# Keys of one residue modulo 16 copied side by side by GpSimd, ahead of the logit products of dilation 16

## The chip, the core and the metric

The kernel runs on one core of one Trainium2 chip. The metric is the device time of one execution in microseconds (us). The kernel before took 2262.62 us, the median of three runs (2255.15 to 2264.13). The profiled execution took 2264.64 us, of which 2262.8 us lie between its first and its last instruction.

## The reference, cut to what matters

One layer of an encoder for 4096 tokens of width 1024. The normalised input is projected; half of the width goes through a gated convolution of width 3, the other half through attention with 8 heads of 64. The attention is what the change touches:

```python
DILATED_CONFIGS = ((128, 1), (512, 4), (2048, 16))   # window, dilation
# for each: query i attends to the keys i + dilation*j, |j| <= 64
logits = einsum('bhnqd,bhnkd->bhnqk', qr, kblk) * dh**-0.5
p = exp(logits + bias - max)
o = p @ v / sum(p)
# the three results are mixed by a softmax over their log-sum-exps
```

For a dilation `d` the sequence is split into `d` residue classes. Within one class the pattern is a band of half-width 64, swept in blocks of 128 queries that see 256 keys (192 at the first and the last block of a class). A class of dilation 16 has 256 tokens, so it is two blocks, and each of them sees 192 keys.

## The kernel before, in words

The kernel has three parts. The first projects x to queries, keys, values and gates, with 512-column matmuls (L385 to L387), and writes them to device memory. The second, from about 793 us to 1903 us, runs the attention together with the convolution's projections, and the third joins the three dilations and multiplies with the output weights.

In the second part the attention is cut into 384 **units**: a pair of heads (4 pairs), a dilation, a quarter (`grp`, 4 of them) and a block of 128 queries (`b`, 8 of them). For each pair of heads 32 units of dilation 16 come first, then 32 of dilation 1 and 32 of dilation 4 (for the last pair, 4 and then 1). Such 32 units in a row are called a **stage** here; there are twelve stages, four of them of dilation 16.

The order of all work is written out by hand: the loop from L1098 issues for each unit, on all engines, a slice of a pipeline, and each engine executes its instructions in that order. In the iteration of unit `u`:

- `p_hi` and `p_lo` (L1026, L1038) split the probabilities of `u` into two f16 parts on ScalarE and VectorE. For even units a DMA transposes them (`tr`, L1048); for odd units TensorE has transposed them before (`tr_pe`, L1019), and the columns that a block of 192 keys leaves empty are zeroed by GpSimd (L994, L1035).
- `exps(u + 1)` on ScalarE (L1003).
- `fill` (L844) issues the convolution's matmuls (L809 to L811, 128x256), so many steps for each unit by a fixed plan (`pers`). The convolution's gate is a GpSimd multiply (L775) that waits for VectorE (L774).
- `av(u - 3)` (L1052) multiplies probabilities and values, 12 matmuls of 64 columns (L1061 to L1063).
- `q_alone(u + 5)` (L968): GpSimd copies the queries of one head of the pair, 64x128, into a tile `qz` whose other half is zero (two copies, L973). The tile was last used by unit `u + 1`, so the copy waits for that unit's products.
- `qk(u + 2)` (L975): four matmuls, L985 and L986 for each head of the pair. The 128 queries are loaded as weights; the keys are the moving operand. L985 takes the packed tile of queries and one part of the keys, L986 takes `qz` and another part of the keys.
- `logits(u + 2)` (L989): VectorE adds the bias and takes the maximum.
- For units of dilation 1 `q_order` (L952) has GpSimd put queries in order (128x256, L958).

Queries and keys of a pair of heads lie in five tiles `qk_t` of 128x4096 f16, filled by transposing DMAs in four chunks of 1024 columns (L615); tiles 0 and 1 hold queries, 2 to 4 keys. Their columns are sorted by residue modulo 4. So the keys of a unit of dilation 4 lie side by side, those of dilation 1 in runs of 32, and those of dilation 16 are read with a step of 4 elements, which is 8 bytes:

```python
step, at = (4, grp * (S // 4) + b // 2) if d == 16 else (1, grp * (S // 4))
U["kc"] = (at + step * (128 * n - (0 if lead else 64)), [[step, U["kn"]]])
```

The queries of dilation 16 have the same step (`U["qc"]`), as weights in L985 and as input of the copies L973.

Of the kernel before, what the change touches and what calls it, by code (L numbers as in the profile page):

```python
# [20 lines left out]
F16 = mybir.dt.float16  # L21
# [8 lines left out]
S = 4096  # L30
# [27 lines left out]
QZB = 4  # L58
# [7 lines left out]
def tile_hybrid_block(  # L66
# [14 lines left out]
    nc = tc.nc  # L81
# [24 lines left out]
    def bank(n, shape, dt=F32):  # L106
        return ps.tile(shape, dt, name=f"bank{n % 8}")
# [497 lines left out]
    pb = phB.enter_context(tc.tile_pool(name="pb", bufs=1))  # L605
    qk_t = [pb.tile([128, S], F16, name=f"qk{j}") for j in range(3)]
# [237 lines left out]
    def fill(n):  # L844
        state["owed"] += n
        while state["owed"] >= 1.0 and not state["done"]:
            state["owed"] -= 1.0
            if bg:
                bg.pop(0)()
            if todo:  # L850
                todo.pop(0)()
            try:
                next(dense)
            except StopIteration:
                state["done"] = True
# [30 lines left out]
    def load_v(pr, g, grp):  # L886
        d = DILS[g]
        vt = pb.tile([128, 9, 256], F16, name="vt", bufs=2)
        up, dn = slice(64, 128), slice(0, 64)
        if d == 16:  # L890
            nc.scalar.dma_start(vt[up, 0:4, :], v_rows(pr, grp, [[16 * VR, 64], [4 * VR, 4], [1, 256]]))
            nc.scalar.dma_start(vt[:, 4:8, :], v_rows(pr, 16 * 64 + grp, [[16 * VR, 128], [4 * VR, 4], [1, 256]]))
            nc.scalar.dma_start(vt[dn, 0:4, :], v_rows(pr, 16 * 192 + grp, [[16 * VR, 64], [4 * VR, 4], [1, 256]]))
        elif d == 4:
            nc.scalar.dma_start(vt[up, 0:8, :], v_rows(pr, grp, [[4 * VR, 64], [512 * VR, 8], [1, 256]]))
            nc.scalar.dma_start(vt[dn, 1:9, :], v_rows(pr, 4 * 64 + grp, [[4 * VR, 64], [512 * VR, 8], [1, 256]]))

            nc.scalar.dma_start(vt[dn, 0, :], v_rows(pr, grp, [[4 * VR, 64], [1, 256]]))
            nc.scalar.dma_start(vt[up, 8, :], v_rows(pr, grp, [[4 * VR, 64], [1, 256]]))
        else:  # L900
            for r in range(4):
                rows = slice(32 * r, 32 * r + 32)
                n = 8 if grp in (0, 3) else 9
                tok = 1024 * grp + (64 if grp == 0 else -64) + r
                nc.scalar.dma_start(vt[rows, int(grp == 0):int(grp == 0) + n, :], v_rows(pr, tok, [[4 * VR, 32], [128 * VR, n], [1, 256]]))
                if n == 8:
                    tok = (S - 128) * (grp == 3) + r
                    nc.scalar.dma_start(vt[rows, 8 * (grp == 3), :], v_rows(pr, tok, [[4 * VR, 32], [1, 256]]))
        return vt
# [3 lines left out]
    units = []  # L913
    for gi, (pr, g, grp) in enumerate(groups):
        d = DILS[g]
        for b in range(8):
            if d == 16:
                n, nb = b % 2, 2
                vidx = (b // 2 + 4 * n, b // 2 + 4 * (1 - n))
            elif d == 4:  # L920
                n, nb, vidx = b, 8, (b, b + 1)
            else:
                n, nb, vidx = 8 * grp + b, 32, (b, b + 1)
            lead, last = n == 0, n == nb - 1
            U = dict(pr=pr, g=g, d=d, grp=grp, gi=gi, b=b, vidx=vidx, kn=256, c0=0)
            if d == 1:

                U["qc"] = (128 * (b % 2), [[1, 128]])
                U["kc"] = (16, [[-16, 2]]) if lead else (32 * n, [[-16, 2]]) if last else (32 * n - 16, [[32, 2]])
                U["kc"][1].extend([[S // 4, 4], [1, 32]])  # L930
                U["b0"] = 256 if lead else 0 if last else 128
                if lead or last:
                    U["vidx"] = (b + 1, b)
            else:
                step, at = (4, grp * (S // 4) + b // 2) if d == 16 else (1, grp * (S // 4))
                U["qc"] = (at + step * 128 * n, [[step, 128]])
                U["kn"] = 256 - 64 * lead - 64 * last
                U["kc"] = (at + step * (128 * n - (0 if lead else 64)), [[step, U["kn"]]])
                U["b0"] = U["c0"] = 64 if lead else 0
            units.append(U)  # L940
    VT, OT, ST, PT = {}, {}, {}, {}
# [4 lines left out]
    def cols(t, at, rows=None):  # L946
        t = t if rows is None else t[rows]
        return bass.AP(tensor=t.tensor, offset=t.offset + at[0], ap=[list(t.ap[0])] + at[1])
# [14 lines left out]
    QZ = [[pb.tile([128, 128], F16, name=f"qz{n}_{i}") for i in range(2)] for n in range(QZB)]  # L963
# [4 lines left out]
    def q_alone(u):  # L968
        U = units[u]
        q_t = QN[u // 2] if U["d"] == 1 else qk_t  # L970
        for i in range(2):
            half = slice(64 * i, 64 * i + 64)
            nc.gpsimd.tensor_copy(QZ[u % QZB][i][half], cols(q_t[i], U["qc"], half))  # L973

    def qk(u):  # L975
        U = units[u]
        if U["b"] == 0:
            OT[U["gi"]] = pb.tile([128, 8, 2, DH + 2], F32, name="ot", bufs=2)
        kn = U["kn"]
        both = bank(3 + u % 2, [128, 2, 256])  # L980
        p = [both[:, i] for i in range(2)]
        qc, kc = U["qc"], U["kc"]
        q_t = QN[u // 2] if U["d"] == 1 else qk_t
        for i in range(2):
            nc.tensor.matmul(p[i][:, 0:kn], cols(q_t[i], qc), cols(qk_t[2 + i], kc), start=True, stop=False)  # L985
            nc.tensor.matmul(p[i][:, 0:kn], QZ[u % QZB][i], cols(qk_t[4], kc), start=False, stop=True)  # L986
        ST[u] = p

    def logits(u):  # L989
# [13 lines left out]
    def exps(u):  # L1003
        U = units[u]
        ot, b, L = OT[U["gi"]], U["b"], ST[u]
        for i in range(2):
            nc.scalar.activation(L[:, i], L[:, i], AF.Exp, scale=-1.0,  # L1007
                                 bias=ot[:, b, i, DH:DH + 1], accum_out=ot[:, b, i, DH + 1:DH + 2])
# [3 lines left out]
    def by_pe(u):  # L1012
        return u % 2 == 1
# [12 lines left out]
    def p_hi(u):  # L1026
        U = units[u]
        if by_pe(u):
            PT[u] = pb.tile([128, 2, 2, 2, 128], F16, name="pt", bufs=PTB)
            nc.scalar.activation(PT[u][:, 0].rearrange("p a b q -> p (a b) q"), ST[u], AF.Copy, scale=P_SCALE)  # L1030
            return
        src = SRC[u // 2 % SRCB]
        c = slice(U["c0"], U["c0"] + U["kn"])
        if U["kn"] < 256:
            nc.gpsimd.memset(src.rearrange("p a b c -> p (a b) c")[:, :, dead(U)], 0.0)  # L1035
        nc.scalar.activation(src[:, 0, :, c], ST[u], AF.Copy, scale=P_SCALE)  # L1036
# [44 lines left out]
    NU = len(units)  # L1081
    start, mid = 112, 184
# [4 lines left out]
    run_tasks(first_loads, 17)  # L1087
    VT[0] = load_v(*groups[0])
    fill(start - 17)
    for u in range(QZB):  # L1090
        q_alone(u)
    for u in range(2):
# [5 lines left out]
    for u in range(NU):  # L1098
        U = units[u]
        p_hi(u)  # L1100
        p_lo(u)
        if u + 1 < NU:
            exps(u + 1)
        if not by_pe(u):
            tr(u)
        fill(pers[u] / 2)
        if u >= LAG:
            av(u - LAG)
        if u + QZB + 2 < NU and units[u + QZB + 2]["d"] == 1 and units[u + QZB + 2]["b"] % 2 == 0:
            q_order(u + QZB + 2)  # L1110
        if u + QZB + 1 < NU:
            q_alone(u + QZB + 1)
        if u + 2 < NU:
            qk(u + 2)
        if u + 3 == NU:
            c_room2()
            sz_load(0)
        if u + 2 < NU:
            logits(u + 2)
        if u + 3 == NU:  # L1120
            c_room4()
        if u > 8 and U["b"] == LAG + 1:
            o_store(U["gi"] - 1)
        if U["b"] == LAG and U["gi"] + 1 < len(groups):
            VT[U["gi"] + 1] = load_v(*groups[U["gi"] + 1])
        fill(pers[u] / 2)
        if u + 1 < NU and by_pe(u + 1):
            tr_pe(u + 1)
        if state["done"]:
            for _ in range(4):  # L1130
                if bg:
                    bg.pop(0)()
        pr = U["pr"]
        if u == 4:
            load_bias(0, 0)
            load_bias(0, 1)
        for a, b, at, rate in CHUNKS:
            p, n = divmod(u - at, 96)
            for n in range(rate * n, min(5, rate * n + rate) if 0 <= p < 3 else 0):
                load_stacks(p + 1, n, a, b)  # L1140
        n = u - LAG
        if n > 0 and n % 32 == 0 and n // 32 <= 9:
            load_bias((n - 32) // 96 + 1, order[0][(n // 32 - 1) % 3])
# [107 lines left out]
```

## Time and profile before

| | us |
|---|---|
| median of three runs | 2262.62 |
| profiled execution | 2264.64 |
| its span, first to last instruction | 2262.8 |
| TensorE matmuls busy | 2152.2 (95%) |
| TensorE weight loads busy | 1577.9 (70%) |
| VectorE busy | 1427.5 (63%) |
| ScalarE busy | 1087.2 (48%) |
| GpSimd busy | 769.4 (34%) |

In the rows, PE is TensorE's matmuls, PEld its weight loads, DVE VectorE, ACT ScalarE, POOL GpSimd, SP SyncE (SPq: what SP's queue issues). Matmuls are pipelined: the duration of a matmul holds its way through the array, so that the distance from one start to the next tells what it costs. PEclk is the share of the full TensorE clock that was granted.

### The profile page before, as it was taken

To read this page: it belongs to the slowest core of one execution; us is meant where nothing else is said; L and a number is where in the kernel's file an instruction comes from. 1 tells how busy PE (TensorE), PEld (TensorE's weight loads), DVE (VectorE), ACT (ScalarE), POOL (GpSimd) and SP (SyncE) were. 2 spreads that over 40 slices of the span, in tenths; PEclk is the share of its full clock that TensorE was granted. 3 is DMA by queue.
4 is the path that set the end of the run, shared out by engine and by line. 5 is a ranking of instruction groups with operands and counts; after the bars stand their busy time and mean duration, and the time that the engine had idled before them with its cause. 6 is when DMAs were issued, how large, how long until landed. Compare 5 with 4: busy or idle time off the path is not lost. (4 is left out here: it accounts for less than half of the span.)

```text
span 2262.8 us, 48552 instructions
## 1 busy us (share of the span) xinstructions
PE 2152.2 (95%) x17726; PEld 1577.9 (70%) x17726; DVE 1427.5 (63%) x4009; ACT 1087.2 (48%) x3128; POOL 769.4 (34%) x1443
## 2 busy tenths in 40 slices
PE   5699999999999989999999999999999998999999
PEld 2244444444444778888888888888888897788887
DVE  4655665656656356766566666676666676787776
ACT  6423333333333156766566666666566675222221
POOL 1132332222233134533344323553233254343332
PEclk9899999999999999999999999999999999999999
DMA  5246467685655775689565896668966558587775
GB/s 178 77 133 169 151 169 171 171 202 144 165 164 142 176 149 134 139 168 191 135 153 116 177 183 153 143 157 170 177 149 132 134 116 223 188 258 257 237 239 188
DMA packets 625005, 377.83 MB, mean 167 GB/s; under 512 B 401281, under 2 KB 567292, under 8 KB 618620
## 3 DMA queue, kind: packets, MB, share of 16 engines
q1 hardware_dynamic: 503396, 304.19, 54.3%
q10 hardware_dynamic: 121368, 70.53, 12.2%
q8 instruction: 139, 2.28, 0.4%
q14 instruction: 102, 0.84, 0.1%
HBM read 174.54 MB, written 110.39 MB: 126 GB/s over the span
## 5 line engine op out<-in xcount | busy, mean ns | idle before, releaser
L809 PE MATMUL bank<-hb,w 128*128 128x256 f16 x2048 | 562.9, 275 | 0.1
L810 PE MATMUL bank<-hb,w 128*128 128x256 f16 x2048 | 560.2, 274 | 0.0
L811 PE MATMUL bank<-hb,w 128*128 128x256 f16 x2048 | 560.1, 274 | 0.0
L998 DVE CUSTOM_DVE_ANT_0 L<-bank,bt,alpha 128x256 f32<-128x256 f32 (+1 forms) x768 | 318.9, 452 | 135.3 <-PE bank L986 89.7
L387 PE MATMUL bank<-wa,hb 128*128 128x512 f16 x1024 | 392.0, 383 | 5.8 <-DMA hb<-xs 5.8
L385 PE MATMUL bank<-wa,hb 128*128 128x512 f16 x1024 | 392.8, 384 | 2.1 <-ACT wa L286 2.1
L386 PE MATMUL bank<-wa,hb 128*128 128x512 f16 x1024 | 392.2, 383 | 0.2 <-DVE wa L287 0.2
L1007 ACT ACTIVATE L<-L,ot 128x256 f32<-128x256 f32 (+1 forms) x768 | 363.6, 476 | 25.8 <-DVE ot L998 23.4
L973 POOL COPY qz<-qk 64x128 f16<-64x128 f16 x512 | 155.3, 303 | 250.9 <-PE bank L986 229.3
L810 PEld LDWEIGHTS <-w 128*128 128x128 f16 x2048 | 203.4, 99 | 29.8 <-issue 0.2
L809 PEld LDWEIGHTS <-w 128*128 128x128 f16 x2048 | 203.4, 99 | 27.4
L811 PEld LDWEIGHTS <-w 128*128 128x128 f16 x2048 | 200.9, 98 | 24.4
L986 PE MATMUL bank<-qk,qz 128*128 128x256 f16 (+1 forms) x768 | 213.3, 298 | 0.0
L238 POOL TENSOR_TENSOR rs_rq<-rs_mq,mhalf 128x8 f32<-128x8 f32 x64 | 107.8, 1684 | 302.9 <-DVE rs_mq L237 302.9
L1042 DVE SCALAR_TENSOR_TENSOR pt<-bank,pt 128x512 f16<-128x512 f32 x192 | 132.5, 690 | 121.6 <-ACT pt L1030 121.0
L1030 ACT ACTIVATE pt<-bank 128x512 f16<-128x512 f32 x192 | 114.6, 597 | 186.4 <-PE bank L1024 181.5
L387 PEld LDWEIGHTS <-hb 128*128 128x128 f16 x1024 | 101.1, 99 | 132.5 <-DMA hb<-xs 9.2
L1061 PE MATMUL bank<-vt,pt 128*128 128x64 f16 x1536 | 175.8, 194 | 14.0 <-DMA pt<-src 9.1
L385 PEld LDWEIGHTS <-hb 128*128 128x128 f16 x1024 | 101.9, 99 | 123.5 <-issue 7.0
L386 PEld LDWEIGHTS <-hb 128*128 128x128 f16 x1024 | 101.1, 99 | 123.8 <-issue 6.3
L1046 DVE SCALAR_TENSOR_TENSOR src<-L,src 128x384 f16<-128x384 f32 (+1 forms) x192 | 127.9, 666 | 90.0 <-ACT src L1036 84.0
L1062 PE MATMUL bank<-vt,pt 128*128 128x64 f16 x1536 | 176.0, 194 | 0.0
(194 smaller groups left out, 4430.9 us busy)
## 6 DMA issues: line engine op xcount, KB each, us to landing
hb<-hT SPq DMA_DIRECT2D x32, 1024.0 KB, 5.8
o_d<-ot ACTq DMA_DIRECT2D x32, 528.0 KB, 5.2
qk<-o_d SPq DMA_DIRECT2D x63, 264.0 KB, 3.7
hT<-hb SPq DMA_DIRECT2D x16, 1024.0 KB, 4.1
wst<-in_w_in_dram SPq DMA_DIRECT2D x64, 256.0 KB, 2.8
qk<-in_x_dram SPq DMA_DIRECT2D x32, 512.0 KB
qk_d<-h SPq DMA_DIRECT2D x128, 96.0 KB, 3.3
vt<-v_d ACTq DMA_DIRECT2D x48, 256.0 KB, 4.0
```

Source lines behind the costliest of these rows:

```text
L385: nc.tensor.matmul(p, hi[:, kt, :], w[:, 0], start=kt == 0, stop=False)
L386: nc.tensor.matmul(p, hi[:, kt, :], w[:, 1], start=False, stop=False)
L387: nc.tensor.matmul(p, lo[:, kt, :], w[:, 0], start=False, stop=kt == KT - 1)
L809: nc.tensor.matmul(pt, w_h, hi[:, :, kt], start=kt == 0, stop=False)
L810: nc.tensor.matmul(pt, w_h, lo[:, :, kt], start=False, stop=False)
L811: nc.tensor.matmul(pt, w_l, hi[:, :, kt], start=False, stop=kt == KT - 1)
L973: nc.gpsimd.tensor_copy(QZ[u % QZB][i][half], cols(q_t[i], U["qc"], half))
L986: nc.tensor.matmul(p[i][:, 0:kn], QZ[u % QZB][i], cols(qk_t[4], kc), start=False, stop=True)
L998: nc.vector.tensor_tensor_reduce(out=L[:, i], in0=p[i][:, 0:kn], in1=bias[:, U["b0"]:U["b0"] + kn], scale=alpha, scalar=BIG, op0=OP.add, o ...
L1007: nc.scalar.activation(L[:, i], L[:, i], AF.Exp, scale=-1.0, bias=ot[:, b, i, DH:DH + 1], accum_out=ot[:, b, i, DH + 1:DH + 2])
L1061: nc.tensor.matmul(p[:, i], hi, v[:, 0:DH], start=j == 0, stop=False)
L1062: nc.tensor.matmul(p[:, i], hi, v[:, DH:], start=False, stop=False)
```

## The change

GpSimd copies the keys of dilation 16, for each residue once, into three tiles `kd` of 128x256 in which they lie side by side. The two units of a residue share them. The even unit makes two of the copies, the odd one the third. The products L985 and L986 of dilation 16 read these tiles with a step of 1; those of the other dilations are as before. There are four sets of three tiles, one for each residue of a quarter. The copies of unit `u + 6` are issued in the iteration of unit `u`, after `q_alone(u + 5)` and before `qk(u + 2)`; those of units 0 to 5 (nine copies) ahead of the first `q_alone`.

```diff
-                U["kc"] = (at + step * (128 * n - (0 if lead else 64)), [[step, U["kn"]]])
+                k0 = 128 * n - (0 if lead else 64)
+                U["kc"] = (k0 if d == 16 else at + k0, [[1, U["kn"]]])
...
+    KD = {}
+
+    def k_dense(u):
+        U = units[u]
+        if U["d"] != 16:
+            return
+        a, r = U["grp"] * (S // 4), U["b"] // 2
+        if U["b"] % 2 == 0:
+            KD[u // 2] = [pb.tile([128, 256], F16, name=f"kd{r}_{j}") for j in range(3)]
+        for j in ((0, 1), (2,))[U["b"] % 2]:
+            nc.gpsimd.tensor_copy(KD[u // 2][j], qk_t[2 + j].rearrange("p (n r) -> p r n", r=4)[:, r, a // 4:a // 4 + 256])
...
+        k_t = KD[u // 2] if U["d"] == 16 else qk_t[2:5]
         for i in range(2):
-            nc.tensor.matmul(p[i][:, 0:kn], cols(q_t[i], qc), cols(qk_t[2 + i], kc), start=True, stop=False)
-            nc.tensor.matmul(p[i][:, 0:kn], QZ[u % QZB][i], cols(qk_t[4], kc), start=False, stop=True)
+            nc.tensor.matmul(p[i][:, 0:kn], cols(q_t[i], qc), cols(k_t[i], kc), start=True, stop=False)
+            nc.tensor.matmul(p[i][:, 0:kn], QZ[u % QZB][i], cols(k_t[2], kc), start=False, stop=True)
...
+    for u in range(6):
+        k_dense(u)
     for u in range(QZB):
         q_alone(u)
...
             q_alone(u + QZB + 1)
+        if u + 6 < NU:
+            k_dense(u + 6)
         if u + 2 < NU:
             qk(u + 2)
```

## Rows read from the trace of the kernel before

**Rows 1.** Busy time by stage (windows), the four stages of dilation 16.

```profile
core 0: us, PE busy (x) PEld busy (x) DVE busy (x) ACT busy (x) POOL busy (x), PEclk, DMA share, GB/s
792.69:890.33 97.64, 88.56 (x958) 74.19 (x957) 53.49 (x194) 54.19 (x195) 36.98 (x119) 0.97 0.65 140
...
1068.80:1162.00 93.20, 91.24 (x1038) 77.45 (x1035) 54.83 (x196) 55.87 (x202) 34.70 (x109) 1.00 0.65 149
...
1344.43:1440.07 95.64, 94.56 (x1074) 81.07 (x1071) 56.30 (x201) 56.25 (x200) 33.46 (x107) 1.00 0.63 141
...
1626.37:1720.38 94.01, 94.01 (x1074) 81.14 (x1071) 55.98 (x201) 56.17 (x204) 31.52 (x103) 1.00 0.63 138
```

**Rows 2.** The same view, a stage of dilation 1.

```profile
890.33:975.41 85.08, 82.82 (x1035) 74.80 (x1032) 61.38 (x199) 59.80 (x201) 40.96 (x95) 1.00 0.70 152
```

**Rows 3.** The waits of TensorE and GpSimd: total us, times, longest us.

```profile
PE bank L1024 <- ACT L L1007: 22.0, 25, 2.9
...
POOL cc L775 <- DVE cc L774: 170.5, 34, 10.4
```

**Rows 4.** TensorE's timeline, one unit of dilation 16: start us, duration us, instruction.

```profile
843.51 0.33 PE L985 MATMUL bank<-qk,qk 128*128 128x192 f16 x1
843.67 0.36 PE L986 MATMUL bank<-qk,qz 128*128 128x192 f16 x1
843.84 0.35 PE L985 MATMUL bank<-qk,qk 128*128 128x192 f16 x1
844.02 0.35 PE L986 MATMUL bank<-qk,qz 128*128 128x192 f16 x1
844.19 0.29 PE L809 MATMUL bank<-hb,w 128*128 128x256 f16 x1
844.32 0.27 PE L810 MATMUL bank<-hb,w 128*128 128x256 f16 x1
```

**Rows 5.** The same view, a first block of a class of dilation 4.

```profile
996.56 0.25 PE L985 MATMUL bank<-qk,qk 128*128 128x192 f16 x1
996.65 0.25 PE L986 MATMUL bank<-qk,qz 128*128 128x192 f16 x1
996.73 0.25 PE L985 MATMUL bank<-qk,qk 128*128 128x192 f16 x1
996.81 0.25 PE L986 MATMUL bank<-qk,qz 128*128 128x192 f16 x1
996.89 0.27 PE L809 MATMUL bank<-hb,w 128*128 128x256 f16 x1
997.00 0.27 PE L810 MATMUL bank<-hb,w 128*128 128x256 f16 x1
```

**Rows 6.** GpSimd's copies, by line: duration ns min/median/max.

```profile
L973 POOL COPY qz<-qk x512: 279/292/832, 790.3 to 1795.7; 64x128 f16<-64x128 f16 x171
...
L958 POOL COPY qn<-qk x128: 602/627/1095, 875.8 to 1884.4; 128x256 f16<-128x256 f16 x128
```

**Rows 7.** GpSimd's timeline: its longest wait at L775 within the four stages.

```profile
1643.43 0.72 POOL L775 TENSOR_TENSOR cc<-cc,gb 128x256 f32<-128x256 f32 x1 [6.20 <-DVE cc L774]
```

**Rows 8.** Line L994: the instructions, and which matmuls waited for it (us, times).

```profile
L994 POOL MEMSET L<- x80: 203/203/205, 794.0 to 1810.9; 128x128 f32 x80
...
  PE bank L1024: 0.8, 1
```

**Rows 9.** The start of the second part: timelines of GpSimd, TensorE and SP.

```profile
790.30 2.71 POOL L973 COPY qz<-qk 64x128 f16<-64x128 f16 x8
...
792.85 0.35 PE L986 MATMUL bank<-qk,qz 128*128 128x192 f16 x1
...
770.72 28.23 SPq L615 DMA_TRANSPOSE qk<-qk_d  x17
...
809.95 0.23 PE L1061 MATMUL bank<-vt,pt 128*128 128x64 f16 x1 [6.54 <-DMA pt<-src]
```

**Rows 10.** VectorE's split of even units: duration ns min/median/max.

```profile
L1046 DVE SCALAR_TENSOR_TENSOR src<-L,src x192: 544/684/1406, 796.3 to 1902.1; 128x512 f16<-128x512 f32 x112, 128x384 f16<-128x384 f32 x80
```

## The prediction, written before the changed kernel was run

> **What bounds the kernel now.** I read the busy time by stage first, because the change touches only the four stages of dilation 16. In them TensorE works 88.56 of 97.64 us, 91.24 of 93.20, 94.56 of 95.64 and 94.01 of 94.01, while VectorE and ScalarE reach some 55 us and GpSimd 32 to 37 [rows 1]. So these stages last as long as TensorE's own work and 12.1 us of idle time in all (9.08 + 1.96 + 1.08 + 0); 6.5 us of that is one wait at the very start [rows 9]. A stage of dilation 1, with 82.82 us of TensorE work, lasts 85.08 us, with VectorE at 61 us [rows 2]: the other engines can follow at a pace that is faster than that of dilation 16 today. The list of waits shows what is next in line: TensorE waits for the exponentials of the unit that it is to transpose (22.0 us in the whole run), and GpSimd stands at the convolution's multiply L775 until VectorE delivers (170.5 us, 34 times) [rows 3].
>
> Then I read the timeline of single units, by the distance from start to start, since a matmul's duration holds the way through the array. A unit of dilation 16 starts its four products at 843.51, .67, .84 and 844.02 and goes on at 844.19: 0.68 us for four matmuls of 192 columns, and the convolution's matmul behind them takes 0.13 us to the next [rows 4]. A block of dilation 4 with the same shape, 192 columns, goes from 996.56 to 996.89: 0.33 us, and the matmul behind it takes 0.11 us [rows 5]. The two differ in the step of the moving keys (4 against 1 elements) and in the step of the queries loaded as weights in L985. But L986, whose weights are the packed tile `qz` in both, is slowed as much as L985 (0.17 against 0.08 us). So it is the keys, as far as two timelines can tell.
>
> **The change, part by part.**
>
> *Products with keys side by side.* Each of the 128 units of dilation 16 (4 pairs of heads x 4 quarters x 8 blocks) gives back 0.68 - 0.33 + 0.02 = 0.37 us on TensorE, 47 us in all. The weights of L985 keep their step. Rows 4 and 5 do not show packed keys beside strided weights, so I bound it: at best nothing is lost; at worst L985's half of the gain goes, 2 x 0.09 x 128 = 23 us. I take nothing, because L985 and L986 have the same distances in rows 4 although only one has strided weights. The range carries a part of that end.
> [...]
>
> *The copies.* 64 residues x 3 = 192 copies of 128x256 on GpSimd. Nearest rows: L973 copies 64x128 in 0.292 us, L958 copies 128x256 in 0.627, at most 1.095 [rows 6]. L973 reads with the same step of 8 bytes in the dilation 16 stages; with twice its columns and a constant part the copy should be 0.5 to 0.6 us. I take 0.55 us: 106 us in all, 26 us in a stage. GpSimd then has 58 to 63 us of work in a stage of some 82 to 86 us. It stays off TensorE's path while it is ahead: the copies of unit u + 6 are issued four iterations before the products that read them, some 10 us.
>
> *What is queued behind them.* GpSimd executes in order. Behind the copies stand the next `q_alone`, the zeroing of L (L994, which `tr_pe` of that unit waits for) and of src (L1035, which the transposing DMA on SP's queue waits for, and behind that `av`). Where GpSimd has stood at L775, 6.20 us in the worst case here [rows 7], it has 2.4 units of backlog, which now hold 2.4 x 1.5 x 0.55 = 2.0 us more. There is one L775 for each 128 channels of a chunk of 256 tokens (64 in all), about five in a stage, so 20 such places. Before, the zeroing of L held TensorE once, for 0.8 us [rows 8]. Bounds: 0, if the slack always covers it, and 20 x 0.8 = 16 us if each place costs what the one did. I take 3 us, near the lower end, since it was seen once in 80.
>
> *A faster TensorE waits more.* The stages come down to 79 to 83 us of TensorE work (88.56 to 94.56 less 11.8). The nearest stage that runs at that pace, rows 2, idles 2.26 us. Four times that is 9.0, against 5.6 us now without the start: 3.4 us are given back. Bounds: the 5.6 us that are there vanish, or they grow by 9.
>
> *The start.* Nine copies, 5 us, come before the first `q_alone`, which began at 790.30; the first L986 at 792.85 would wait until about 796, 3 us. But at 809.95 TensorE waits 6.54 us for the first transposed probabilities, and SP's queue was busy with the loads of the keys until 799 (770.72 + 28.23) [rows 9]. A delay of 3 us ahead of that wait comes out of it. I take 0; if the cover is gone, 3 us.
>
> *VectorE.* Its split of even units reads two operands from SBUF, and it took 1.406 us at most where 0.684 is usual [rows 10]. With 16 such splits a stage, 0.1 us more each is 2 us of VectorE in a stage with over 20 us to spare. Taken as 0.
>
> **Sum.** -47 + 3 + 3.4 = -41 us. The profiled execution took 2264.64 us, so the same execution would take 2224; the median of the runs shown is 2 us lower than the profiled one, which gives **2222 us**. Lower end: all 47 us, and the 5.6 us of waits gone: 2262.6 - 52.6 = 2210. Upper end: 2222 + 13 (all L775 places) + 3 (start) + 6 (waits at the upper bound) = 2244; a strided weight load that costs half of its bound lies inside that.
>
> **The rivals.**
>
> 1. *The copies buy nothing:* a step of 8 bytes is free for the moving keys, and the 0.17 us of rows 4 come from something else in the units of dilation 16, the strided weights or a neighbour on SBUF. Then the products stay as they are, and the stages, as long as before, hide the copies: 2263 us. Against it stands L986, slow in rows 4 and fast in rows 5 with the same weights. 4%.
> [...]
>
> 2. *Half is given back:* GpSimd, behind at every L775 and with more in its queue, delays zeroing, transposes and queries in most units; each of the 64 transposes by TensorE in these stages waits some 0.3 us, 19 us in place of 3 and 0.05 us a unit more for late `av`: 2222 + 16 + 6 = 2244 us, at the end of the range. For it: GpSimd's long waits in rows 3. Against: one wait of TensorE for it in rows 8. 13%.
>
> 3. [...]
> [...] 4%.
>
> **Chances.** Forecast 79%, half given back 13%, nothing 4%, slower 4%. The measurement of this kernel can tell a difference of about 0.5%, 11 us, from none: faster by more than that means below 2251 us. Nearly all of the first two cases lies there: faster 0.91, within 0.5% 0.05, slower 0.04.
>
> **What the profile after would show.** L985 and L986 of dilation 16 with starts 0.08 us apart; a new GpSimd line with 192 copies of 0.5 to 0.6 us; the four stages at 82 to 87 us, the other eight as before; TensorE's waits for L994 and for the exponentials a few us longer. I am wrong if the distances stay above 0.12 us (the keys' step was not it, or the strided weights set the pace), if TensorE waits for the copies or for `qz` in the stages, or if stages of dilation 1 and 4 change by more than a microsecond or two.

## The result, and the profile after

| | us |
|---|---|
| before, median of four runs, the three named above and a fourth (2255.15 to 2264.13) | 2260.5 |
| after, median of four runs (2230.64 to 2235.53) | 2233.56 |
| after, profiled execution, and its span | 2230.64, 2228.8 |

The ratio is 0.9882, with a 95% interval of 0.9857 to 0.9906: the change is worth 27 us of the forecast 41. The profiled execution before (2264.64 us) was slower than all four runs and the one after is the fastest of its four, so the two profiles lie 34 us apart; where sums over the two traces stand below, it is this 34 that they add up to.

Behind the edit the line numbers are up by 15: L994 is L1009 here, L1007 is L1022, L1024 is L1039, L1061 is L1076; L973 is L974.

The first view is again the busy time by stage: the four stages of dilation 16, with the sum that the view prints, and ahead of the sum a stage of dilation 1 from a second answer.

```profile
core 0: us, PE busy (x) PEld busy (x) DVE busy (x) ACT busy (x) POOL busy (x), PEclk, DMA share, GB/s
791.80:883.10 91.30, 79.38 (x959) 70.39 (x958) 53.82 (x194) 53.54 (x195) 55.09 (x168) 0.96 0.68 150
883.10:968.20 85.10, 82.84 (x1035) 74.73 (x1032) 61.41 (x199) 59.86 (x201) 41.00 (x95) 1.00 0.71 152
1061.10:1146.40 85.30, 80.75 (x1037) 72.95 (x1034) 54.49 (x196) 54.84 (x200) 51.99 (x151) 1.00 0.77 164
1328.10:1415.90 87.80, 83.75 (x1075) 76.79 (x1072) 56.03 (x201) 55.81 (x200) 49.66 (x148) 1.00 0.68 152
1601.90:1688.60 86.70, 84.11 (x1076) 76.75 (x1072) 56.10 (x201) 56.07 (x204) 47.05 (x144) 1.00 0.71 149
...
sum 351.10, PE 327.99 PEld 296.87 DVE 220.44 ACT 220.27 POOL 203.80; mean PE 82.00 PEld 74.22 DVE 55.11 ACT 55.07 POOL 50.95
```

Against [rows 1] the four stages went from 380.5 us to 351.1, by 29.4 of the 34. TensorE's busy time in them fell from 368.4 to 328.0, by 40.4, and what it idles rose from 12.1 to 23.1, by 11.0. The stage of dilation 1 lasts 85.10 us as in [rows 2].

The next view is TensorE's timeline of one unit of dilation 16, to be read against [rows 4] and [rows 5].

```profile
1061.11 0.25 PE L1000 MATMUL bank<-kd,qk 128*128 128x192 f16 x1
1061.19 0.25 PE L1001 MATMUL bank<-kd,qz 128*128 128x192 f16 x1
1061.28 0.25 PE L1000 MATMUL bank<-kd,qk 128*128 128x192 f16 x1
1061.36 0.25 PE L1001 MATMUL bank<-kd,qz 128*128 128x192 f16 x1
1061.44 0.27 PE L809 MATMUL bank<-hb,w 128*128 128x256 f16 x1
1061.55 0.27 PE L810 MATMUL bank<-hb,w 128*128 128x256 f16 x1
```

The four products take 0.33 us from start to start and the matmul behind them 0.11, to the digit what dilation 4 took. L1000, which still loads its queries with the step of 4, is as fast as L1001 with the packed `qz`.

The new line on GpSimd (L987) and who waited for it:

```profile
L987 POOL COPY kd<-qk x192: 400/411/812, 789.4 to 1674.3; 128x256 f16<-128x256 f16 x192
...
who waited for it (us, times):
  DVE L L1013: 2.5, 3
  DVE src L1061: 1.4, 1
```

A copy takes 0.411 us, not 0.55, and TensorE waits for none of them. What TensorE does wait for in the whole run (total us, times, longest us, as in [rows 3]):

```profile
PE bank L1039 <- ACT L L1022: 25.2, 25, 2.5
...
PE bank L1076 <- DMA pt<-src: 16.6, 9, 6.6
...
PE bank L1076 <- ACT ot L1079: 2.5, 4, 1.0
PE bank L1039 <- POOL L L1009: 2.1, 3, 1.6
...
PE bank L1001 <- POOL qz L974: 0.9, 1, 0.9
```

The same view cut to the four stages tells where the 11 us more of idle time stand: transposed probabilities that are late (`pt<-src`, transposed by DMA) 6.5 us before and 12.3 after, exponentials 4.8 and 7.5, GpSimd's zeroing 0.8 and 2.2, and the first unit's queries 0 and 0.9. That makes 22.9 after against 12.1. The profile of run 1 below, the same kernel once more, has 9.2, 8.1, 1.3 and 0.9, together 19.5: the growth repeats, and its split between the causes moves by some 3 us from one profile to the next.

One of the waits for exponentials, followed to its cause. First TensorE's wait, then ScalarE's timeline ahead of it (ACTq: what ScalarE's queue issues):

```profile
1142.41 0.88 PE L1039 MATMUL bank<-identf,L 128*128 128x128 f32 x4 [2.16 <-ACT L L1022]
```

```profile
1137.34 0.47 ACTq L908 DMA_DIRECT2D vt<-v_d  x1
...
1137.84 1.06 ACTq L905 DMA_DIRECT2D vt<-v_d  x1
1138.93 0.47 ACTq L908 DMA_DIRECT2D vt<-v_d  x1
1139.44 0.44 ACTq L905 DMA_DIRECT2D vt<-v_d  x1
1139.92 0.46 ACTq L908 DMA_DIRECT2D vt<-v_d  x1
1140.42 0.43 ACTq L905 DMA_DIRECT2D vt<-v_d  x1
1140.89 0.46 ACTq L908 DMA_DIRECT2D vt<-v_d  x1
1141.40 0.52 ACT L1051 ACTIVATE src<-L 128x384 f16<-128x384 f32 x1 [3.79 <-DMA vt<-v_d]
...
1141.83 0.44 ACT L1022 ACTIVATE L<-L,ot 128x192 f32<-128x192 f32 x1
```

From 1137.6 us on, for the 3.79 us in the brackets of the line at 1141.40, ScalarE does nothing but issue loads of values for the next quarter (`load_v`, L905 and L908), one after the other, and its exponentials stand in line behind them. This engine is busy 55 of 85 us in such a stage. The prediction had looked at that share and not at the queue.

### The profile page after: what moved, and what is told of

Its sections match the earlier page's. It is cut to its first block, busy times and chain, and to the rows that moved or that the text cites. A ratio compares the mean times of both kernels' runs of the same rounds, so it can differ in the third digit from the quotient of the medians.

```text
span 2228.8 us, 48736 instructions
## 1 busy us (share of the span) xinstructions
PE 2109.8 (95%) x17726; PEld 1559.6 (70%) x17726; DVE 1432.0 (64%) x4009; ACT 1085.4 (49%) x3128; POOL 844.9 (38%) x1635
## 5 line engine op out<-in xcount | busy, mean ns | idle before, releaser
L1022 ACT ACTIVATE L<-L,ot 128x256 f32<-128x256 f32 (+1 forms) x768 | 363.6, 476 | 25.9 <-DVE ot L1013 24.7
L974 POOL COPY qz<-qk 64x128 f16<-64x128 f16 x512 | 158.4, 309 | 161.3 <-PE bank L1001 143.9
L1076 PE MATMUL bank<-vt,pt 128*128 128x64 f16 x1536 | 175.7, 193 | 19.2 <-DMA pt<-src 16.6
L1061 DVE SCALAR_TENSOR_TENSOR src<-L,src 128x384 f16<-128x384 f32 (+1 forms) x192 | 131.2, 683 | 92.0 <-ACT src L1051 85.6
L1077 PE MATMUL bank<-vt,pt 128*128 128x64 f16 x1536 | 175.9, 193 | 0.0
L1078 PE MATMUL bank<-vt,pt 128*128 128x64 f16 x1536 | 175.9, 193 | 0.0
```

Source lines behind the costliest of these rows:

```text
L1022: nc.scalar.activation(L[:, i], L[:, i], AF.Exp, scale=-1.0, bias=ot[:, b, i, DH:DH + 1], accum_out=ot[:, b, i, DH + 1:DH + 2])
L1076: nc.tensor.matmul(p[:, i], hi, v[:, 0:DH], start=j == 0, stop=False)
L1077: nc.tensor.matmul(p[:, i], hi, v[:, DH:], start=False, stop=False)
L1078: nc.tensor.matmul(p[:, i], lo, v[:, 0:DH], start=False, stop=j == 1)
```

## The experiments

**Three theories.** All take the faster products as given. **A**: GpSimd's copies take back what is missing, by delaying what stands behind them or by getting in VectorE's way. **B**: the copies cost nothing; a TensorE that is done sooner waits for work of other engines that did not get faster, exponentials and transposes. **C**, formed after the first runs: within B, the exponentials are late because ScalarE's queue stands in issuing the value loads.

**1. The change once more**, with nothing altered, for a base on the same chip as the next three.

> The changed kernel once more, as the yardstick for the runs beside it. Both theories expect 2230 to 2236 us, some 27 us under the kernel before (a ratio near 0.988).

2237.57 us against 2261.13, ratio 0.9886 [0.9864, 0.9907]. The gain repeats.

**2. Keys side by side without copies.** The kernel before, with dilation 16 reading other keys that happen to lie side by side.

```diff
-                U["kc"] = (at + step * (128 * n - (0 if lead else 64)), [[step, U["kn"]]])
+                U["kc"] = (grp * (S // 4) + 128 * n - (0 if lead else 64), [[1, U["kn"]]])
```

> No copies at all; the products of dilation 16 read 192 neighbouring columns of the old tiles, which are other keys. TensorE has the same work as in the changed kernel, GpSimd the same as before. Theory A (what was given back, some 20 of 47 us, is GpSimd's extra queue: late zeroing, late transposes, the start): most of it comes back, 2215 to 2224 us. Theory B (given back because TensorE, being faster, runs into the latency of exponentials and transposing DMAs, whatever GpSimd does): 2228 to 2236 us, as the changed kernel.

2233.3 us, ratio 0.9877 [0.9854, 0.9899], nearly the interval of the change itself. TensorE's waits in this run:

```profile
PE bank L1024 <- ACT L L1007: 26.6, 26, 2.8
...
PE bank L1061 <- DMA pt<-src: 13.7, 7, 7.4
```

They are those of the changed kernel though GpSimd copies nothing. Theory A falls; B stands.

**3. The copies alone.** The changed kernel with its copies, which no product reads.

```diff
-        k_t = KD[u // 2] if U["d"] == 16 else qk_t[2:5]
+        k_t = qk_t[2:5]
...
-                U["kc"] = (k0 if d == 16 else at + k0, [[1, U["kn"]]])
+                U["kc"] = (at + step * (128 * n - (0 if lead else 64)), [[step, U["kn"]]])
```

> The copies are made as in the change, but the products read the keys with the step of 4 as before; nothing reads the copies. Theory A: the copies alone delay TensorE, 2266 to 2280 us. Theory B: with the old slow products there is slack enough, 2258 to 2265 us, as before, save up to 3 us at the start.

2259.39 us (12 runs), ratio 0.9998 [0.9983, 1.0013]: 192 copies, 192 x 0.411 = 79 us of GpSimd's time, cost nothing that can be measured.

**4. What a step costs.** The kernel before, with another step of the keys or of the queries in each quarter of a stage of dilation 16 (16 of each matmul at each value). It computes with other keys, and in some quarters other queries.

```diff
+                if d == 16:
+                    a0 = grp * (S // 4)
+                    U["kc"] = (a0, [[1, 192]])
+                    if pr == 0:
+                        U["kc"] = (a0, [[(1, 2, 3, 4)[grp], 192]])
+                    elif pr == 1:
+                        U["kc"] = (0, [[(5, 6, 8, 16)[grp], 192]])
+                    elif pr == 2:
+                        U["qc"] = (a0, [[(1, 2, 4, 7)[grp], 128]])
+                    elif grp < 3:
+                        U["kc"] = (a0, [[[8, 96], [1, 2]], [[16, 48], [1, 4]], [[16, 24], [1, 8]]][grp])
+                    else:
+                        U["qc"], U["kc"] = (a0, [[1, 128]]), (a0, [[4, 192]])
```

> No copies; in each quarter of the dilation 16 stages the keys (or the query weights) are read in another pattern, so they are other keys and queries: key steps 1, 2, 3, 4 (first pair of heads), 5, 6, 8, 16 (second), query weights with steps 1, 2, 4, 7 and keys side by side (third), keys in runs of 2, 4 and 8 elements with gaps, and packed queries with keys of step 4 (fourth). Distance from start to start for 192 columns. [...] My theory, that any step at which neighbouring keys share no smaller unit halves the rate: step 1 and perhaps 2 at 0.08, 4 to 16 at 0.17 us; weights with a step cost nothing; runs of 2 halve it too or less, runs of 8 not.

Groups of one line (L999, the L986 of before) by quarter (count, then busy us and mean ns of one; the idle time last): steps of 2, 4, 8 and 16 elements, then runs of 2 in 8 and of 4 in 16.

```profile
L999 PE MATMUL bank<-qk,qz 128*128 128x192 f16 x16 | 3.4, 248 | 0.0
...
L999 PE MATMUL bank<-qk,qz 128*128 128x192 f16 x16 | 5.6, 353 | 0.0
...
L999 PE MATMUL bank<-qk,qz 128*128 128x192 f16 x16 | 8.3, 522 | 0.0
...
L999 PE MATMUL bank<-qk,qz 128*128 128x192 f16 x16 | 8.4, 527 | 0.0
...
L999 PE MATMUL bank<-qk,qz 128*128 128x192 f16 x16 | 5.6, 353 | 0.0
...
L999 PE MATMUL bank<-qk,qz 128*128 128x192 f16 x16 | 3.4, 249 | 0.0
```

These matmuls overlap: with a step of 8 one lasts 0.51 us and the next starts 0.34 us after it, and in the timeline after, with packed keys, it is 0.25 and 0.08, some 0.17 us longer than the distance in both. So the distances from start to start tell what a unit's four products cost. Of a unit with a step of 8, the first product and the matmul behind the four, 1.35 us apart:

```profile
1125.73 0.51 PE L998 MATMUL bank<-qk,qk 128*128 128x192 f16 x1
...
1127.08 0.29 PE L809 MATMUL bank<-hb,w 128*128 128x256 f16 x1
```

This distance, worked out from the timeline as the median of each quarter:

| keys (elements of 2 bytes) | four products, us | 16-byte lines in 192 keys |
|---|---|---|
| step 1 | 0.33 | 24 |
| step 2 | 0.35 | 48 |
| step 3 | 0.52 | 72 |
| step 4 | 0.68 | 96 |
| step 5 | 0.84 | 120 |
| step 6 | 1.01 | 144 |
| step 8 | 1.35 | 192 |
| step 16 | 1.37 | 192 |
| runs of 2 in 8 | 0.67 | 96 |
| runs of 4 in 16 | 0.35 | 48 |
| runs of 8 in 16 | 0.33 | 24 |
| step 4, queries packed | 0.67 | 96 |

The time follows the number of 16-byte lines that the keys touch, 1.77 ns a line for each matmul (192 x 1.77 = 340 ns, four times that is 1.36 us), and never falls below the 0.33 us of packed keys. Steps of 8 and 16 cost nearly the same, as both touch a line for each key, and runs of 2 in 8 cost what a step of 4 does. The theory names no size for the unit that neighbouring keys share; that it is 16 bytes comes out of two pairs: counted in lines of 8 bytes, a step of 4 would cost as much as one of 8 (0.68 and 1.35 us here), and counted in lines of 32, a step of 16 twice as much as one of 8 (1.37 and 1.35). With packed keys, queries with a step of 1, 2, 4 and 7 as weights give 0.33, 0.33, 0.33 and 0.35 us. So what the change removed was the cost of the keys' step, and of it alone. (The kernel as a whole, 2255.06 us in one run, averages over these quarters and says nothing.)

**5. Value loads issued by SyncE.** Theory C: the changed kernel, where `load_v` issues from SP's queue. All nine calls are altered alike.

```diff
-                nc.scalar.dma_start(vt[rows, int(grp == 0):int(grp == 0) + n, :], v_rows(pr, tok, [[4 * VR, 32], [128 * VR, n], [1, 256]]))
+                nc.sync.dma_start(vt[rows, int(grp == 0):int(grp == 0) + n, :], v_rows(pr, tok, [[4 * VR, 32], [128 * VR, n], [1, 256]]))
```

> The changed kernel with the loads of the values issued by SP's queue instead of ScalarE's. Theory C (the exponentials that TensorE waits for are late because ScalarE's queue has just issued up to eight loads, some 4 us): TensorE's waits for the exponentials fall from 25.2 us to under 10, and the time by 10 to 15 us, to 2220 to 2227 us. Theory D (ScalarE or VectorE are late by their own work): the waits stay above 20 us and the time at 2230 to 2238. Rival E: SP's queue, which issues the transposes, becomes late instead: TensorE's waits for transposed probabilities grow from 16.6 us by as much as is won.

2206.8 us, ratio 0.976 [0.9748, 0.9773]: 27 us below the changed kernel, more than expected. TensorE's waits:

```profile
PE bank L1076 <- DMA pt<-src: 15.0, 7, 6.8
...
PE bank L1039 <- POOL L L1009: 11.5, 5, 4.5
PE bank L1039 <- ACT L L1022: 4.2, 2, 2.9
```

The waits for exponentials fall from 25.2 us to 4.2, as C has it, and those for transposed probabilities do not grow (16.6 and 15.0). The zeroing of L comes up in their place. Stretches in which ScalarE's arithmetic stands still while its queue issues DMAs for over 1.5 us go from 37 in the second part, with 84 us of issuing, to 3 with 7 us. Not all of the 27 us are visible waits (in the second part of the kernel they fall from 45.8 to 35.1 us); a wait that ends under the matmul ahead of it is not in this list. Counting from start to start finds these too. Taken as **lateness** of a matmul what its distance from the one before exceeds the usual distance of such a pair (the median in the changed kernel's second part; what matmuls lose where the granted clock is 0.5, 0.21 us from start to start for 256 columns in place of 0.11, is kept apart), TensorE's transposes of probabilities, which wait for exponentials and zeroing, are late by 45.7 us in the second part of the changed kernel and by 17.9 here.

**6. The same edit on the kernel before.**

> The same edit in the kernel before, without the copies. If TensorE's waits for the exponentials are the common second limit, the kernel before wins about as much of its 22.0 us, 10 to 13 us in all: 2248 to 2252 us, and f1 lies 30 us or more under it. If the wait for ScalarE's queue is what took back the gain of the change alone, this kernel wins less than 5 us (2256 to 2262) and f1 more.

2240.1 us, ratio 0.991 [0.9896, 0.9924], on the same chip as run 5. The edit is worth 20 us without the packed keys and 27 with them; the packed keys are worth 33.3 us with ScalarE's queue free (2240.1 - 2206.8), and 27 with it occupied. The lateness of TensorE's transposes agrees: it falls from 38.2 to 17.9 us with the edit here, by 20.3, and from 45.7 to 17.9 there, by 27.8. So the queue took some 6 us of the change's gain, and 20 us that have nothing to do with the change. By the intervals of the three ratios the 6 are uncertain by about as much; the lateness says 7.5, and the four stages alone say 5.4 (34.8 - 29.4), by the sums that follow. They are over the four stages of dilation 16, first of this run and then of run 5:

```profile
sum 378.90, PE 368.22 PEld 315.54 DVE 220.11 ACT 223.53 POOL 136.90; mean PE 92.06 PEld 78.88 DVE 55.03 ACT 55.88 POOL 34.22
```

```profile
sum 344.10, PE 324.85 PEld 298.88 DVE 221.69 ACT 220.87 POOL 206.94; mean PE 81.21 PEld 74.72 DVE 55.42 ACT 55.22 POOL 51.73
```

The stages shorten by 34.8 us here and by 29.4 between the two kernels of the study; TensorE's busy time by 43.4 and 40.4; the idle time grows by 8.6 and 11.0. In run 6 TensorE waits 7.7 us for transposed probabilities in the whole run, in run 5 15.0.

**7. Products of probabilities and values one unit later**, to give the transposing DMAs more time.

```diff
-PTB = 4
+PTB = 5
...
-LAG = 3
+LAG = 4
...
-            KD[u // 2] = [pb.tile([128, 256], F16, name=f"kd{r}_{j}") for j in range(3)]
+            KD[u // 2] = [pb.tile([128, 256], F16, name=f"kd{r % 2}_{j}") for j in range(3)]
...
-            k_dense(u + 6)
+            k_dense(u + 4)
...
-        if u > 8 and U["b"] == LAG + 1:
+        if u > 8 and U["b"] == LAG:
```

> The changed kernel with the products of probabilities and values four units behind in place of three (one more buffer for the transposed probabilities; to make room two sets of key copies in place of four, made four units ahead). If waits for late transposes are a limit of their own, those outside the start (10 us) vanish and the time falls by 5 to 10 us, to 2225 to 2230. If another wait ends last in their place, the time stays at 2230 to 2238.

2322.97 us, ratio 1.0275 [1.0262, 1.0289]: a miss, slower by 63 us than before. TensorE's waits for the transposes fall to 3.6 us, but another wait takes their place, that for ScalarE's copy of the previous result (L1079). The list's line, and a stretch of ScalarE's timeline:

```profile
PE bank L1076 <- ACT ot L1079: 94.5, 46, 7.9
```

```profile
1002.23 0.39 ACTq L1094 DMA_DIRECT2D o_d<-ot  x1
1002.66 0.66 ACTq L895 DMA_DIRECT2D vt<-v_d  x1
1003.35 1.48 ACTq L896 DMA_DIRECT2D vt<-v_d  x1
1004.88 0.75 ACTq L898 DMA_DIRECT2D vt<-v_d  x1
1005.66 0.61 ACTq L899 DMA_DIRECT2D vt<-v_d  x1
1006.32 0.60 ACT L1045 ACTIVATE pt<-bank 128x512 f16<-128x512 f32 x1 [3.87 <-issue]
```

The edit had put the stores of one quarter and the value loads of the next into one iteration, so it made ScalarE's blocks longer: the stretches counted in run 5 are 46 with 173 us here, where the changed kernel has 37 with 84, and the longest issues for 5.6 us in place of 4.0. TensorE also waited 6.0 us for the copies of keys, which are made only four units ahead here. And it was granted 0.5 of its clock for 92 us of the second part (14 in the changed kernel): that cost some 29 us in place of 5, of the 91 us by which this part is longer. The run agrees with C, and leaves open what a longer lag alone would do.

**8. The start in another order.** The changed kernel, with the first copies put between the first queries.

```diff
-    for u in range(6):
-        k_dense(u)
     for u in range(QZB):
+        if u % 2 == 0:
+            k_dense(u)
+            k_dense(u + 1)
...
+    for u in (4, 5):
+        k_dense(u)
```

> The changed kernel with the first copies of keys between the first copies of queries, instead of all ahead of them, so that the first unit's copies come first. My prediction's step on the start: a delay there comes out of the wait for the first transpose, so no change, 2230 to 2238 us, with the wait at the start longer by what the delay was. Rival: the start costs 2 to 4 us, and the time falls to 2229 to 2234.

2232.83 us, ratio 0.9881 [0.9867, 0.9896]: no difference that can be seen, and both expectations have room for this time. A gain of 2 to 3 us is not excluded: in this run's profile 14.3 us pass from the first product to the end of TensorE's wait for the first transposed probabilities, 17.1 in the changed kernel and 16.3 in run 1.

**9. Run 2 with the value loads on SP's queue**: other keys that lie side by side, no copies. Its edit is those of runs 2 and 5 together.

> As f1 (values loaded by SP's queue, keys side by side), but without the copies: the products read neighbouring columns of the old tiles, which are other keys. It prices the copies where ScalarE's queue no longer covers them. If GpSimd's copies are free, 2204 to 2210 us, as f1 (2206.8). If they hold TensorE by late zeroing (11.5 us of waits for L1009 in f1), 2195 to 2201.

2203.6 us, ratio 0.9742 [0.9728, 0.9756]; with the copies it was 2206.8, ratio 0.976, so with ScalarE's queue free the copies cost 3.2 us by the medians, which overlapping intervals do not tell from nothing; the time lies between the two expectations. The zeroing of L holds TensorE here too, without a single copy of keys ahead of it:

```profile
PE bank L1024 <- POOL L L994: 15.8, 4, 7.5
```

**10. The gate's multiply later.** Run 5's kernel, in which GpSimd's L775 comes 12 steps of the plan after VectorE's last part, so that GpSimd need not stand there.

```diff
+        def gate():
             nc.gpsimd.tensor_tensor(cc[:, :w], cc[:, :w], gt[:, :w], op=OP.mult)
...
-        return [f0, f1, f2] + [lambda: None] * 10 + [f3]
+        return [f0, f1, f2] + [lambda: None] * 12 + [gate] + [lambda: None] * 8 + [f3]
```

> f1 with the convolution's gate multiply (L775) put 12 steps later in the hand-written order, so that GpSimd does not stand still in front of it while zeroing and copies queue up. If GpSimd's in-order queue is the next limit, TensorE's waits for L1009 fall from 11.5 us to under 3 and the time to 2195 to 2200. If the gate's place does not matter, 2204 to 2210.

2201.8 us, ratio 0.9737 [0.9723, 0.975], about 5 us below run 5, with intervals that just overlap. The waits for the zeroing are 9.6 us in place of 11.5. That lies between the two expectations, and settles neither.

**11. The stores on SP's queue too.** Run 5's kernel with `o_store` (L1090 to L1094) issued by SyncE.

```diff
-            nc.scalar.dma_start(dap(o_d[g], grp * R + base, [[4 * R, 128], [512 * R, 8], [1, RW]]), src)
+            nc.sync.dma_start(dap(o_d[g], grp * R + base, [[4 * R, 128], [512 * R, 8], [1, RW]]), src)
```

> f1 with the attention's stores also issued by SP's queue. ScalarE's queue has 1 to 2 of these issues (some 0.6 us each) for every 8 units. If every DMA issue on ScalarE's queue costs TensorE, a few us less than f1, 2200 to 2205. If short ones are covered, 2204 to 2210; if SP's queue is full, its transposes come late and the time rises above 2210.

2216.47 us, ratio 0.9804 [0.9785, 0.9823], 10 us above run 5. TensorE's waits for the copies of results (L1079) rise from 3.3 to 18.8 us. Moving the stores as well as the loads off ScalarE's queue is worse than moving the loads alone. TensorE's waits for transposed probabilities fall (15.0 to 9.5), so the late transposes that were expected of a full SP queue do not show. What makes the copies of results late was not found out.

**12. Bias tables one copy at a time.** In run 5 a zeroing for which TensorE waited 1.93 us, until 992.50 us, stood behind GpSimd's building of the next bias tables, which itself had waited for a load:

```profile
987.10 1.48 POOL L877 COPY bt<-wst 128x128 f32<-128x128 f32 x4 [6.83 <-DMA wst<-bv_d]
...
988.73 1.98 POOL L877 COPY bt<-wst 128x128 f32<-128x128 f32 x4
...
992.24 0.20 POOL L1009 MEMSET L<- 128x128 f32 x1
```

Run 10's kernel, with those copies put off by six units and then issued one in each unit.

```diff
+        def copy(i, j, c):
...
+        later.extend([lambda: None] * 6)
...
-                nc.gpsimd.tensor_copy(bt0[:, i, j].rearrange("p (r n) -> p r n", r=4), src)
...
+                later.append(lambda i=i, j=j, c=c: copy(i, j, c))
...
+        if later:
+            later.pop(0)()
```

> g1 with the copies that spread a new bias table for dilation 1 (L877, L879), before which GpSimd stood 3 to 7 us for the table's load, put 6 units later and one to a unit. If TensorE's remaining waits for zeroing (9.6 us in g1, 4 times) come from these copies and not from the copies of keys, they fall under 2 us and the time by 5 to 9 us, to 2193 to 2197. If the copies of keys cause them, they stay and the time is 2199 to 2205, as g1.

2187.01 us against 2259.16, ratio 0.9685 [0.9665, 0.9705]: 72 us below the kernel before and some 14 below run 10, where 5 to 9 were expected. Of these 14, 10 are lateness of TensorE's transposes (11.4 us in run 10, 1.1 here). The wait for the zeroing is gone from TensorE's list, where the transposes remain:

```profile
PE bank L1085 <- DMA pt<-src: 17.8, 9, 7.4
```

So the long waits for GpSimd came from the bias tables, not from the keys' copies. This is the best version of the study; it contains the change, and beats both kernels.

## Why the prediction was right or wrong

**Products: right.** 0.37 us for each of 128 units, 47 us, was forecast. Summed over the four stages from start to start, the products went from 86.3 to 44.3 us (0.9 of that is the hold at the first unit), and the matmuls behind them lost 2.6: together some 45. The bound of 23 us for strided weights was not needed: runs 2 and 4 and the timeline after show packed keys beside strided queries at 0.33 us a unit. Rival 1 falls with it. In run 4 a step of 4 elements, with two keys in each 16-byte line, costs 0.68 us where packed keys cost 0.33, and with four keys in a line (a step of 2, or runs of 4 in 16) it is 0.35 us.

**The copies: right that they are hidden, too dear by a third.** 0.411 us in place of 0.55, 79 us in place of 106, with nothing on the path that runs 2 and 3 can measure; run 9 leaves room for some 3 us once the loads have moved. The longest copy took 0.812 us, and the slower kernel, given 4%, did not come.

**What is queued behind them: small, as forecast.** 3 us were taken. TensorE's waits for GpSimd in the stages rose by 1.4 us for the zeroing and 0.9 at the start, and run 2, with no copies, has the same time within its interval.

**A faster TensorE waits more: the term that was sized wrong.** The prediction took 3.4 us, from what a stage of dilation 1 idles, four times, and bounded it by a growth of 9. (The stages' TensorE work comes down to 77 us at the low end by its own sum, 88.56 - 11.8, not 79.) Measured are 11.0 us more of idle time in the four stages, and with the products some 45 us cheaper and the stages 29.4 shorter, some 16 us were given back there. As lateness, from start to start, the parts can be told. TensorE's transposes, which wait for exponentials and zeroing, are late by 15.6 us in the four stages, 8.5 before. The products of probabilities and values, which wait for transposed probabilities, are late by 13.5, 6.7 before, and the first products by 1.0. Stretches at half the clock cost 2.0, 1.5 before: the granted clock was 0.5 from 807.0 to 813.9 us, and TensorE had stood idle from 802.3 to 808.9. In the profiles of runs 1, 2 and 8, with the same products, the first of these is 15.7 to 17.1, the second 10.2 to 11.5, and the clock costs 3.4 to 4.9. So late exponentials, and a little zeroing, gave back 7 to 9 us, and late transposed probabilities 3 to 7.

The model behind the step, that stages with the same TensorE load idle alike, was the error: the mean load does not show bursts in the other queues. One burst is shown to count, some 4 us of value loads in ScalarE's queue (3.79 us in the stretch shown). With it removed from both kernels the change is worth 33 us, not 27 (runs 5 and 6), so it accounts for about 6 of the some 14 us that the forecast was too good by, and the lateness of TensorE's transposes is then 17.9 us in either kernel. What remains lies mostly with the late transposed probabilities (7.7 us of waits in run 6, 15.0 in run 5; but two profiles of the changed kernel have 16.6 and 12.4). Why they are late is open. The two longest such waits in the stages, after the start, follow transposing DMAs issued 8.2 and 8.4 us before, where 3.4 is the median to landing; the one run aimed at them, run 7, was spoilt by its own side effect.

That the time fell into the stated range was in part luck: the range's upper end, 2244 us, held 13 us for GpSimd's places at L775, which were not needed. With the upper bound of this term alone it would have been 2228, and 2233.56 was measured.

**The start: right in sum.** Forecast at 0. The first L1001 was held only 0.9 us in place of 3. From the first product to the end of the wait for the first transposed probabilities 17.1 us pass, 17.3 before, so the hold cost nothing; the wait itself lasts 6.62 us where it was 6.54 [rows 9], as the products ahead of it are shorter too:

```profile
808.93 0.23 PE L1076 MATMUL bank<-vt,pt 128*128 128x64 f16 x1 [6.62 <-DMA pt<-src]
```

Run 8, with another order of the first copies, shows no gain beyond its interval.

**VectorE: right.** Its busy time in the stages is 220.4 us, 220.6 before. It waited for the copies 3.9 us in the whole run, and run 3 prices that at nothing.

**Rival 2 was as near in size as the forecast, and wrong in the cause.** It put the time at 2244 us, 10 above the measured one where the forecast was 12 below, with half of the gain given back because GpSimd is behind. Some 16 of 45 us were given back, but mostly by late exponentials, with ScalarE's queue ahead of them, and by late transposed probabilities; the long waits for GpSimd, which came up once the loads had moved, belong to the bias tables (run 12) and stand in run 6 without the change (10.0 us).

**Signs named ahead.** Distances of 0.08 us, four stages between 85 and 91 us where 82 to 87 were named, the stages of dilation 1 and 4 unchanged (all but the last add up to 639.2 us, 639.4 before), TensorE's waits a few us longer: all but the stages' length as foretold. The start apart, TensorE waited neither for copies nor for `qz`.

## What to carry to other kernels

Before packing a moving operand, count the 16-byte lines that its columns touch: in run 4, with f16, a step of 2 was nearly free (0.35 us a unit against 0.33), from 3 to 8 the price rose in proportion (0.52 to 1.35 us), and a step of 16 cost what one of 8 did (1.37); strided weights cost nothing up to a step of 4 (0.33 us). When a stage on the critical engine is to get faster, do not take its new idle time from a mean: look in the timelines of the engines that feed it for bursts of a few microseconds, and among them count the DMAs that a compute engine issues, since no table of busy time here holds them. An engine busy 55 of 85 us held the path, and moving its loads to another queue gained as much as the change itself (27 us each).

## What the runs showed of the hardware that was not expected

- In run 4 TensorE's moving operand was read at 1.77 ns for each 16-byte line touched once that exceeded the matmul's own 82 ns for 192 columns; a step of 16 elements cost hardly more than one of 8 (1.37 and 1.35 us a unit).
- GpSimd copied 128x256 with a step of 8 bytes in 0.411 us; the row that it was sized by, half of the columns in 0.292 us, had suggested 0.5 to 0.6, and L958 takes 0.627 for the same size [rows 6].
- Issuing a DMA held ScalarE's queue for 0.43 to 1.06 us each in the stretch shown, and up to 1.48 in run 7, and no arithmetic of ScalarE ran in those 3.79 and 3.87 us.
- A transposing DMA landed after 3.4 us in the median, and after 10.4 at most; before the change it was 2.9 and 10.2.
- While TensorE stood idle from 802.3 to 808.9 us its granted clock fell to 0.5, at 807.0; it stayed there until 813.9, and the 256-column matmuls then started 0.21 us apart in place of 0.11.
